# Moving the samples' chunk behind the first prompt chunk in the scans of a hybrid decoder layer

## The chip, the cores and the metric

One core of one Trainium2 chip. The metric is the device time of one execution in microseconds (us); lower is better. The kernel is written in Python with a tile framework: the program states tiles, pools and instructions, and a planner in the framework works out the order of the instructions on each engine.

## What is computed

One inference step of one decoder layer for 512 prompt tokens and 8 x 8 sample tokens that share the weights: a half-step SwiGLU FFN, one combined input projection, a Mamba-2 branch (SSD) and an attention branch side by side, a merge with an output projection, and a second half-step FFN. The change is in the SSD branch. Cut to it, the reference reads:

```python
xc, conv_new = causal_conv(xbc, conv_prev, conv_w, conv_b)      # depthwise, SiLU
acs = jnp.cumsum(dtc * A, axis=2)                               # inside a chunk of 128 tokens
cb = jnp.einsum('bclgn,bcsgn->bclsg', Cc, Bc)
y_diag = jnp.einsum('bclsgr,bcsgrp->bclgrp', cb[..., None] * decay, xdt)
states = jnp.einsum('bclgn,bclgr,bclgrp->bcgrpn', Bc, jnp.exp(acs[:, :, -1:] - acs), xdt)
# h = chunk_decay * h + states, from chunk to chunk
y_off = jnp.einsum('bclgn,bcgrpn,bclgr->bclgrp', Cc, h_prev, jnp.exp(acs))
y = (y_diag + y_off) + d_skip * x;  then y * silu(z) and a group RMSNorm
```

The prompt is four chunks of 128 tokens whose states form a chain. The samples are 8 sequences of 8 new tokens each with a state of its own from memory; the kernel takes all 64 tokens as one more chunk.

## The kernel before

All activations lie transposed, features on the 128 partitions and 576 tokens (512 prompt, 64 sample) on the free axis. Matrices are multiplied in three passes of split operands (`mm3`, L212, L215, L216: high x high, low x high, high x low), in two halves of 288 tokens. A weight tile is loaded by SP (`stage`, L164, four buffers), split by ScalarE (`whi`, L176) and by VectorE or GpSimd (`wlo`, L177). Results go to two PSUM banks `acc`; other PSUM rings are `tr`, `mm` and `pv`, two banks each.

The SSD branch goes in four groups g of eight heads. For each group `group_in(g)` projects six tiles (B, C and four tiles of x) and applies the conv in `conv_tile`: VectorE takes a projection out of `acc` (L1189, L1194, L1196), TensorE transposes the last columns into the same bank (L1202) and ScalarE copies them out (`tt`, L1204), VectorE adds the taps (L1215) and multiplies by the gate (L1217), GpSimd does so for the samples (L1220). `group_scan(g)` is the scan, and `group_out(g)` projects its result (L1474, L1477, L1481 take it out of `acc`). The emission order is scan g, `group_in(g+1)`, some gate tiles (`gate_tile`, evicted at L598; three behind scan 0, five behind scan 3), `group_out(g)`. The planner takes instructions by this order among those that are ready by its own planned times, so projections of the neighbouring groups stand between the pieces of a scan.

In a scan, `chunk(c, hst)` handles a chunk; c is 0 to 3 for the prompt and 4 for the samples:

- TensorE multiplies B and C (L1348) and VectorE masks it (L1349).
- For two sets of four heads, SP loads the cumulated decays to all partitions (`ab`, L1354, four buffers); ScalarE makes the ramps and the exponential (`dk`, L1359, L1360, four buffers) and VectorE multiplies by the masked scores (L1361). For chunks 1 to 3 ScalarE and GpSimd also make the factors for the state (L1363, L1364).
- TensorE transposes x (L1370) into an `mm` bank and VectorE scales it twice, `xdt` (L1373) and `xde` (L1375). TensorE transposes B (L1377) into another `mm` bank; ScalarE copies it (`bt`, L1380), or, for the samples, `operands` splits both and stores them with four transfers on ScalarE's queue for the last FFN (L1330 to L1340).
- TensorE does the product (L1386) and, for chunks 1 to 3, that with the state so far (L1390), both into a `pv` bank; VectorE adds the skip (L1392). For the prompt, `gate` loads z (L1309, one buffer), multiplies on GpSimd (L1311) and squares.

`carry` multiplies `xde` and `bt` (L1401, an `mm` bank) into the new state `hst` (L1404 for chunk 0, L1406 and L1407 behind it). `state` multiplies the samples' old states, loaded by SP (`hT`, L1413, three buffers), for each c (L1415). At the end of a scan the samples' part is put together (L1440, L1442) and gated, and `halves` splits the result for `group_out` (L1324, L1325).

Of the kernel before, what the change touches and what calls it, by code (L numbers as in the profile page):

```python
# [89 lines left out]
def ap3(ap, offset, dims):  # L90
    return bass.AP(tensor=ap.tensor, offset=ap.offset + offset, ap=[list(d) for d in dims])


def build(ctx, tc, A, O):
# [3 lines left out]
    def tl(pool, shape, dt=F32, tag=None, bufs=None):  # L98
        uid[0] += 1
        kw = {} if bufs is None else {"bufs": bufs}  # L100
        return pool.tile(shape, dt, tag=tag, name=f"{tag}_{uid[0]}", **kw)
# [23 lines left out]
    def C(n, rows=P):  # L125
        o, w = COFF[n]
        return cst[:rows, o - P:o - P + w]

    def bank(tag, bufs=None):
        return tl(sp, [P, 512], tag=tag, bufs=bufs)  # L130

    def tr():
        return bank("tr", 2)

    def sm():
        return bank("mm", 2)

    def pv():
        return bank("pv", 2)
# [1103 lines left out]
    with qyp:  # L1243
        with pool("yhl", reuse_waits="tile") as yhp:

            yhl = []
            for n, y in enumerate(yt):
                c = G.tensor_copy(y[:, NP:], ys[:, n // 4, n % 4, :])
# [32 lines left out]
    with pool("ssd", side="right", reuse_waits="tile") as wk:  # L1281
# [13 lines left out]
        def group_scan(g, bT, cT, xg):  # L1295
# [10 lines left out]
            def gate(o0, n):  # L1306

                zt = tl(xz, [P, 4, P], tag="zt", bufs=1)[:, :, :n]
                nc.sync.dma_start(out=zt, in_=zD[:, 4 * g:4 * g + 4, o0:o0 + n])  # L1309
                yv = xg[:, :, o0:o0 + n]  # L1310
                G.tensor_tensor(yv, yv, zt, ALU.mult)  # L1311
                q = tl(tp, [P, 4, P], tag="sq", bufs=1)[:, :, :n]
                act(q, yv, AF.Square)
                G.tensor_tensor(q[:, :2, :], q[:, :2, :], q[:, 2:, :], ALU.add)
                G.tensor_tensor(ysq[:, o0:o0 + n], q[:, 0, :], q[:, 1, :], ALU.add)

            def halves(half):

                for i in range(4):
                    if half == 0:  # L1320
                        yhl.append((tl(wo, [P, NT], F32R, tag="ygh", bufs=4), tl(wo, [P, NT], F32R, tag="ygl", bufs=4)))
                    w = P1[:, 24 + 4 * g + i:25 + 4 * g + i]
                    hi, lo = yhl[i][0][:, hs(half)], yhl[i][1][:, hs(half)]
                    act(hi, xg[:, i, hs(half)], AF.Copy, scale=w)  # L1324
                    V.scalar_tensor_tensor(lo, xg[:, i, hs(half)], w, hi.bitcast(F32), ALU.mult, ALU.subtract)  # L1325

            def operands(x, bp):

                xh = tl(wk, [NS, 512], F32R, tag="x4", bufs=3)
                act(xh, x, AF.Copy)  # L1330
                xl = tl(wk, [NS, 512], F32R, tag="x4", bufs=3)
                V.tensor_tensor(xl, x, xh.bitcast(F32), ALU.subtract)
                bh = tl(wk, [NS, P], F32R, tag="cbm", bufs=2)
                act(bh, bp, AF.Copy)
                bl = tl(wk, [NS, P], tag="cbm", bufs=2)
                V.tensor_tensor(bl, bp, bh.bitcast(F32), ALU.subtract)
                nc.scalar.dma_start(out=upxD[g, 0], in_=xh.bitcast(F32))
                nc.scalar.dma_start(out=upxD[g, 1], in_=xl.bitcast(F32))
                nc.scalar.dma_start(out=upbD[g, 0], in_=bh.bitcast(F32))
                nc.scalar.dma_start(out=upbD[g, 1], in_=bl)  # L1340

            def chunk(c, hst):

                n = P if c < 4 else NS
                o0 = c * P

                cbm = tr()
                mm(cbm[:n, :n], lhsT=bT[:, o0:o0 + n], rhs=cT[:, o0:o0 + n], start=True, stop=True)  # L1348
                V.tensor_tensor(cbm[:n, :n], cbm[:n, :n], C("mT") if c < 4 else C("smT", NS), ALU.mult)  # L1349
                abs_, dks = [], []  # L1350
                for r0 in (0, 4):
                    ab = tl(wk, [P, 4, P], tag="ab", bufs=4)
                    abv = ab[:n, :, :n]
                    nc.sync.dma_start(out=abv, in_=ap3(cumD, (g * 8 + r0) * NT + o0, [(0, n), (NT, 4), (1, n)]))  # L1354
                    dk = tl(wk, [P, 4, P], tag="dk", bufs=4)
                    dv = dk[:n, :, :n]
                    for r in range(4):
                        a0 = 64 + g * 8 + r0 + r
                        act(dv[:, r, :], abv[:, r, :], AF.Relu, bias=TT[c][:n, a0:a0 + 1], scale=-1.0)  # L1359
                    act(dv, dv, AF.Exp, scale=-1.0)  # L1360
                    V.tensor_tensor(dv, dv, cbm[:n, :n].unsqueeze(1).to_broadcast([n, 4, n]), ALU.mult)  # L1361
                    if 0 < c < 4:
                        act(ab, ab, AF.Exp)  # L1363
                        G.tensor_tensor(ab, ab, cT[:, o0:o0 + P].unsqueeze(1).to_broadcast([P, 4, P]), ALU.mult)  # L1364
                    abs_.append(ab)
                    dks.append(dk)

                t = sm()
                for i in range(4):
                    nc.tensor.transpose(t[:n, i * P:(i + 1) * P], xg[:, i, o0:o0 + n], ident)  # L1370
                xdt = tl(wk, [P, 8, 64], tag="xdt", bufs=2)
                tv = t[:n].rearrange("s (r p) -> s r p", p=64)
                V.tensor_tensor(xdt[:n], tv, TT[c][:n, g * 8:(g + 1) * 8].unsqueeze(2).to_broadcast([n, 8, 64]), ALU.mult)  # L1373
                xde = tl(wk, [P, 8, 64], tag="xde" if c < 4 else "x4", bufs=1 if c < 4 else 3)
                V.tensor_tensor(xde[:n], tv, wdec[:n, c, g * 8:(g + 1) * 8].unsqueeze(2).to_broadcast([n, 8, 64]), ALU.mult)  # L1375
                t = sm()
                nc.tensor.transpose(t[:n, :P], bT[:, o0:o0 + n], ident)  # L1377
                if c < 4:
                    bt = tl(wk, [P, P], tag="bt", bufs=1)
                    act(bt[:n], t[:n, :P], AF.Copy)  # L1380
                else:
                    bt = operands(xde.rearrange("s r p -> s (r p)")[:NS], t[:NS, :P])
                yb = pv()
                for r in range(8):
                    ov = yb[(r % 2) * 64:(r % 2 + 1) * 64, (r // 2) * n:(r // 2 + 1) * n]
                    own = mm(ov, lhsT=xdt[:n, r, :], rhs=dks[r // 4][:n, r % 4, :n], start=True, stop=not 0 < c < 4)  # L1386
                    if r == 0:
                        owns.append(own)
                    if 0 < c < 4:
                        mm(ov, lhsT=hst[:, r, :], rhs=abs_[r // 4][:, r % 4, :], start=False, stop=True)  # L1390
                for i in range(4):
                    V.scalar_tensor_tensor(xg[:, i, o0:o0 + n], xg[:, i, o0:o0 + n], dsk[:, 4 * g + i:4 * g + i + 1],  # L1392
                                           yb[:, i * n:(i + 1) * n], ALU.mult, ALU.add)
                if c < 4:
                    gate(o0, n)
                return xde, bt

            def carry(c, hst, xde, bt):

                s = sm()  # L1400
                mm(s, lhsT=bt, rhs=xde.rearrange("s r p -> s (r p)"), start=True, stop=True)  # L1401
                hn = tl(wk, [P, 8, 64], tag="hst", bufs=2)
                if c == 0:
                    act(hn.rearrange("n r p -> n (r p)"), s, AF.Copy)  # L1404
                else:
                    G.tensor_tensor(hn, hst, decb[:, c, g * 8:(g + 1) * 8].unsqueeze(2).to_broadcast([P, 8, 64]), ALU.mult)  # L1406
                    V.tensor_tensor(hn.rearrange("n r p -> n (r p)"), hn.rearrange("n r p -> n (r p)"), s, ALU.add)  # L1407
                return hn

            def state(h, i, ob):  # L1410

                hT = tl(wk, [P, 512], tag="hT", bufs=3)
                nc.sync.dma_start(out=hT, in_=hTD[h, 4 * g + i])  # L1413
                for b in range(4):
                    mm(ob[b * 32:(b + 1) * 32, :P], lhsT=cz[:, 4 * h + b, :], rhs=hT[:, b * P:(b + 1) * P], start=h == 0, stop=h == 1)  # L1415

            chunk(4, None)
            oo = tl(wk, [P, 512], tag="oo", bufs=1)
            hst = None
            for c in range(4):  # L1420
                hst = carry(c, hst, *chunk(c, hst))
                ob = pv()
                for h in range(2):
                    state(h, c, ob)
                act(oo[:, c * P:(c + 1) * P], ob[:, :P], AF.Copy)
                if c == 2 and g < 3:
                    halves(0)
# [159 lines left out]
```

## Time and profile before

| | |
|---|---|
| median of 3 runs | 1837.36 us (1836.68 to 1840.5) |
| profiled execution, its own time | 1829.29 us |
| its span, first to last instruction | 1827.4 us |
| granted TensorE clock, mean | 1.00 |
| TensorE busy (PE) | 1798.5 us, 98% |
| weight loads busy (PEld) | 1713.3 us, 94% |
| VectorE, ScalarE, GpSimd busy | 1014.7, 758.1, 630.6 us |

A row of the profile names the source line, the engine, the operation and the tiles. PE is TensorE's matmuls, PEld its weight loads, which overlap them; DVE is VectorE, ACT ScalarE, POOL GpSimd, and SPq, ACTq are the queues on which transfers are issued. Matmuls are pipelined, so a busy PE is not PE at its peak, and the distance between two starts says more than a matmul's own length. A matmul of plain f32 operands stands as two records.

### The profile page before, as it was taken

What the parts mean: (1) busy time and instruction counts of PE and PEld (TensorE: products, weight loads), DVE (VectorE), ACT (ScalarE), POOL (GpSimd) and SP (SyncE); (2) the same over time, 40 slices, a digit from 0 to 9 for tenths busy, and PEclk for the clock granted to TensorE, in tenths of its full rate; (3) what the DMA queues carried; (4) which work ended last, traced back from release to release, by engine and by line L of the source; (5) the groups of instructions that cost most, each with busy time, mean ns of one, the idle gap of its engine ahead of it and who ended that gap; (6) DMA issues with size and microseconds to landing.
All of it is one profiled execution on the core that took longest, in us unless ns stands there. A gap on an engine that the chain in (4) does not pass through costs nothing.

```text
span 1827.4 us, 38776 instructions
## 1 busy us (share of the span) xinstructions
PE 1798.5 (98%) x15315; PEld 1713.3 (94%) x15315; DVE 1014.7 (56%) x2259; ACT 758.1 (41%) x1598; POOL 630.6 (35%) x724
## 2 busy tenths in 40 slices
PE   8999999999999999999999999999999999999999
PEld 7999999999999888888998888888999999999998
DVE  4643334434426777775728857686675444444542
ACT  4333223334324565564427555555333333123322
POOL 0433002312322455453325454848452322002210
PEclk9999999999999999999999999999999999999999
DMA  5544443444546688774356554454473434543342
GB/s 164 161 120 138 129 134 109 124 137 133 120 132 197 201 243 240 244 231 158 89 164 183 153 139 112 124 151 138 153 215 93 127 116 130 152 139 110 111 124 66
DMA packets 297739, 269.72 MB, mean 148 GB/s; under 512 B 55084, under 2 KB 262108, under 8 KB 297404
## 3 DMA queue, kind: packets, MB, share of 16 engines
q1 hardware_dynamic: 229712, 184.16, 35.7%
q10 hardware_dynamic: 57844, 46.10, 8.2%
q0 software_dynamic: 10000, 36.97, 6.4%
q8 instruction: 121, 1.98, 0.5%
q14 instruction: 62, 0.51, 0.1%
HBM read 223.72 MB, written 38.73 MB: 144 GB/s over the span
## 4 chain that ended last, share of the span: by engine, by line
PE 88%; DVE 5%; DMA 3%; ACT 1%; issue 1%; POOL 1%; ACTq 0%; DVEq 0%; SPq 0%; POOLq 0%
PE acc L212 17%; PE acc L215 16%; PE acc L216 16%; PE pv L212 8%; PE pv L215 8%; PE pv L216 8%; PE tr L990 2%; PE tr L977 1%; PE mm L913 1%; PE pv L1386 1%; PE pv L944 1%; PE mm L931 1%; DVE kf L1215 1%; PE mm L1401 1%; PE pv L1028 1%
## 5 line engine op out<-in xcount | busy, mean ns | idle before, releaser
L176 ACT ACTIVATE whi<-stage 128x512 fp32r<-128x512 f32 (+2 forms) x474 | 294.3, 622 | 687.2 <-PE acc L215 589.1
L212 PE MATMUL acc<-xh,whi 128*128 128x288 f32 x1792 | 539.4, 301 | 11.1 <-DVE xr L1189 4.8
L215 PE MATMUL acc<-xl,whi 128*128 128x288 f32 x1792 | 530.4, 296 | 0.0
L216 PE MATMUL acc<-xh,wlo 128*128 128x288 f32 x1792 | 529.3, 295 | 0.0
L177 DVE TENSOR_TENSOR wlo<-stage,whi 128x512 fp32r<-128x512 f32 (+1 forms) x373 | 262.3, 703 | 257.1 <-ACT whi L176 235.0
L212 PEld LDWEIGHTS acc<-xh,whi 128*128 128x128 f32 x1792 | 336.4, 188 | 17.7 <-DVE xr L1189 7.2
L215 PEld LDWEIGHTS acc<-xl,whi 128*128 128x128 f32 x1792 | 336.6, 188 | 1.3 <-issue 1.2
L216 PEld LDWEIGHTS acc<-xh,wlo 128*128 128x128 f32 x1792 | 336.2, 188 | 0.9 <-issue 0.7
L353 POOL TENSOR_TENSOR u<-u,s 128x288 f32<-128x288 f32 x88 | 82.3, 936 | 433.9 <-DVE u L352 378.2
L177 POOL TENSOR_TENSOR wlo<-stage,whi 128x512 fp32r<-128x512 f32 (+1 forms) x101 | 133.9, 1326 | 276.3 <-ACT whi L176 243.3
L212 PE MATMUL pv<-xh,whi 128*128 128x288 f32 (+1 forms) x720 | 213.3, 297 | 0.6 <-ACT xh L227 0.6
L215 PE MATMUL pv<-xl,whi 128*128 128x288 f32 (+1 forms) x720 | 211.7, 294 | 0.0
L216 PE MATMUL pv<-xh,wlo 128*128 128x288 f32 (+1 forms) x720 | 211.6, 294 | 0.0
L212 PEld LDWEIGHTS pv<-xh,whi 128*128 128x128 f32 (+1 forms) x720 | 134.2, 186 | 1.2 <-ACT xh L227 0.8
L215 PEld LDWEIGHTS pv<-xl,whi 128*128 128x128 f32 (+1 forms) x720 | 134.1, 186 | 1.2
L216 PEld LDWEIGHTS pv<-xh,wlo 128*128 128x128 f32 (+1 forms) x720 | 134.0, 186 | 0.2
L212 PE MATMUL pv<-hh,whi 128*128 128x288 f32 x352 | 105.7, 300 | 0.0
L215 PE MATMUL acc<-hl,whi 128*128 128x288 f32 x352 | 104.1, 296 | 0.0
L212 PE MATMUL acc<-hh,whi 128*128 128x288 f32 x352 | 104.1, 296 | 0.0
L215 PE MATMUL pv<-hl,whi 128*128 128x288 f32 x352 | 104.1, 296 | 0.0
L216 PE MATMUL acc<-hh,wlo 128*128 128x288 f32 x352 | 104.1, 296 | 0.0
L216 PE MATMUL pv<-hh,wlo 128*128 128x288 f32 x352 | 103.7, 295 | 0.0
(370 smaller groups left out, 3560.1 us busy)
## 6 DMA issues: line engine op xcount, KB each, us to landing
stage<-in_w_in_dram SPq DMA_DIRECT2D x52, 512.0 KB
stage<-in_ffn_w_up_dram SPq DMA_DIRECT2D x44, 512.0 KB
stage<-in_ffn_w_gate_dram SPq DMA_DIRECT2D x43, 512.0 KB
stage<-in_ffn_w_down_dram SPq DMA_DIRECT2D x40, 512.0 KB
h<-in_state_ssm_dram SPq DMA_DIRECT2D x64, 256.0 KB
hTD<-hT ACTq DMA_DIRECT2D x32, 256.0 KB
pb<-pastD SPq DMA_DIRECT2D x32, 256.0 KB
ab<-cumD SPq DMA_DIRECT2D x32, 256.0 KB
```

Of the source, the lines that this page charges most:

```text
L176: act(hi, view, AF.Copy)
L177: e.tensor_tensor(lo, view, hi.bitcast(F32), ALU.subtract)
L212: begin = mm(out, lhsT=hi, rhs=a, start=first and i == 0, stop=False)
L215: mm(out, lhsT=hi, rhs=b, start=False, stop=False)
L216: end = mm(out, lhsT=lo, rhs=a, start=False, stop=last and i == n - 1)
L353: G.tensor_tensor(u, u, sil[half], ALU.mult)
L913: mm(s[:, :n], lhsT=q, rhs=ks[2 * self.p + e][:, :n], start=hl == 0, stop=hl == 1)
L931: nc.tensor.transpose(t[:, j * P:(j + 1) * P], lt[:, j * P:(j + 1) * P], ident)
L944: mm(self.ob[o:o + 32, i * P:(i + 1) * P], lhsT=vtok[j][:, v0:v0 + 32], rhs=self.pts[e][:, j * P:(j + 1) * P], start=j == 0, stop=j == i)
L977: nc.tensor.transpose(t[:, i * P:(i + 1) * P], kk[:, i, p * P:(p + 1) * P], ident)
L990: mm(s[kv * 32:(kv + 1) * 32, :], lhsT=self.q(kv), rhs=self.kT[kv // 2], start=True, stop=True)
L1028: mm(ob[kv * 32:(kv + 1) * 32, :64], lhsT=self.pt[:, i * P + kv * 32:i * P + (kv + 1) * 32], rhs=vv[:, i, kv * 64:(kv + 1) * 64], start=jq ...
```

## The change

The call for the samples' chunk is moved in each of the four scans: instead of ahead of the loop over the prompt's chunks it stands inside, behind `chunk(0)` and its `carry`, and ahead of the first pair of `state` calls. `chunk` and `carry` themselves are unchanged.

```diff
-            chunk(4, None)
             oo = tl(wk, [P, 512], tag="oo", bufs=1)
             hst = None
             for c in range(4):
                 hst = carry(c, hst, *chunk(c, hst))
+                if c == 0:
+                    chunk(4, None)
                 ob = pv()
                 for h in range(2):
                     state(h, c, ob)
```

## Rows read from the trace of the kernel before

**Rows 1.** The page: its part 1 (busy time of each engine, share of the span, instructions), and the first line of its part 4, which is the chain that ended last, by engine.

```profile
PE 1798.5 (98%) x15315; PEld 1713.3 (94%) x15315; DVE 1014.7 (56%) x2259; ACT 758.1 (41%) x1598; POOL 630.6 (35%) x724
...
PE 88%; DVE 5%; DMA 3%; ACT 1%; issue 1%; POOL 1%; ACTq 0%; DVEq 0%; SPq 0%; POOLq 0%
```

**Rows 2.** The view of windows: for each stretch of the span (us) its length, then busy time of PE, PEld, DVE, ACT and POOL with their numbers of instructions, granted clock, DMA share and GB/s. A stretch ahead of the scans, the four scans, and the first scan's dense part.

```profile
100.00:500.00 400.00, 399.17 (x3035) 396.86 (x3033) 158.37 (x296) 136.42 (x249) 90.99 (x95) 1.00 0.44 128
960.00:1310.00 350.00, 339.08 (x2807) 303.96 (x2806) 254.28 (x551) 200.02 (x488) 198.87 (x227) 1.00 0.50 143
970.00:1010.00 40.00, 39.30 (x379) 33.63 (x379) 37.98 (x73) 35.43 (x95) 29.18 (x31) 1.00 0.66 187
```

**Rows 3.** The waits of PE from 880 to 1320 us: who waited for whom, us in total, times, longest. The two largest.

```profile
PE acc L212 <- DVE xr L1189: 4.4, 7, 2.2
PE acc L212 <- ACT tt L1204: 3.7, 8, 1.4
```

**Rows 4.** The timeline of PE in the second scan (start us, us, engine, line, operation, out<-in, number merged): the product of the samples' chunk (64*64), the pieces of the first prompt chunk behind it, and projection matmuls between them.

```profile
1047.55 0.33 PE L1386 MATMUL pv<-dk,xdt 64*64 64x64 f32 x2
...
1049.37 0.29 PE L216 MATMUL acc<-ygh,wlo 128*128 128x288 f32 x1
1049.59 0.67 PE L1386 MATMUL pv<-dk,xdt 64*64 64x64 f32 x14
1050.19 0.33 PE L1377 MATMUL mm<-ident,bT 128*128 128x128 f32 x1
1050.28 0.38 PE L212 MATMUL acc<-ygh,whi 128*128 128x288 f32 x1
1050.50 0.30 PE L215 MATMUL acc<-ygl,whi 128*128 128x288 f32 x1
...
1052.05 0.87 PE L1386 MATMUL pv<-dk,xdt 128*64 128x128 f32 x10
...
1057.26 1.02 PE L1401 MATMUL mm<-xde,bt 128*128 128x512 f32 x2
...
1060.88 0.66 PE L1370 MATMUL mm<-ident,xg 128*128 128x128 f32 x4
```

**Rows 5.** The timelines of ACT and, in the last row, of POOL in the second scan.

```profile
1050.07 2.16 ACT L1359 ACTIVATE dk<-ab,TT 128x128 f32<-128x128 f32 x7 [1.23 <-PE pv L1386]
1052.13 0.26 ACT L1380 ACTIVATE bt<-mm 128x128 f32<-128x128 f32 x1
...
1059.08 0.59 ACT L1404 ACTIVATE hst<-mm 128x512 f32<-128x512 f32 x1
...
1058.15 2.54 POOL L1364 TENSOR_TENSOR ab<-ab,cT 128x512 f32<-128x512 f32 x2
```

**Rows 6.** Groups of instructions by line and form from 955 to 1330 us, for the forms of the samples' chunk (64 partitions or 64 columns), all four scans: VectorE's, then ScalarE's. Number, busy us, mean ns of one, idle time before them and what ended it.

```profile
L1332 DVE TENSOR_TENSOR x<-x,x 64x512 fp32r<-64x512 f32 x4 | 3.9, 976 | 0.0
...
L1392 DVE SCALAR_TENSOR_TENSOR xg<-xg,dsk,pv 128x64 f32<-128x64 f32 x16 | 3.4, 268 | 0.1
...
L1361 DVE TENSOR_TENSOR dk<-dk,tr 64x256 f32<-64x256 f32 x8 | 2.9, 399 | 0.0
...
L1375 DVE TENSOR_TENSOR x<-mm,wdec 64x512 f32<-64x512 f32 x4 | 2.7, 676 | 0.0
L1373 DVE TENSOR_TENSOR xdt<-mm,TT 64x512 f32<-64x512 f32 x4 | 2.7, 673 | 0.0
...
L1359 ACT ACTIVATE dk<-ab,TT 64x64 f32<-64x64 f32 x32 | 8.7, 336 | 12.7 <-DMA ab<-cumD 12.7
...
L1360 ACT ACTIVATE dk<-dk 64x256 f32<-64x256 f32 x8 | 3.3, 409 | 0.1
```

**Rows 7.** The timeline of PE, rows with idle time ahead of them (in brackets, with what ended it), at the heads and ends of the scans.

```profile
973.12 0.40 PE L212 MATMUL acc<-xh,whi 128*128 128x288 f32 x1 [0.70 <-DVE xr L1189]
...
1013.07 0.40 PE L212 MATMUL acc<-xh,whi 128*128 128x288 f32 x1 [2.21 <-DVE xr L1189]
...
1128.62 0.40 PE L212 MATMUL acc<-xh,whi 128*128 128x288 f32 x1 [0.58 <-ACT tt L1204]
...
1197.05 0.40 PE L212 MATMUL acc<-xh,whi 128*128 128x288 f32 x1 [1.37 <-ACT tt L1204]
...
1228.00 0.41 PE L212 MATMUL acc<-xh,whi 128*128 128x288 f32 x1 [0.33 <-DVE xr L1189]
```

**Rows 8.** Timelines of the first scan: PE's products of the first and the third prompt chunk, VectorE's decays of the third chunk, a split and an eviction at the scan's end; and of the last scan: VectorE's last splits and last eviction of a gate tile.

```profile
981.28 0.66 PE L1386 MATMUL pv<-dk,xdt 128*64 128x128 f32 x8
...
994.93 0.45 PE L1386 MATMUL pv<-dk,xdt 128*64 128x128 f32 x4
...
989.43 1.27 DVE L1361 TENSOR_TENSOR dk<-dk,tr 128x512 f32<-128x512 f32 x2
...
1006.60 2.65 DVE L1325 SCALAR_TENSOR_TENSOR ygl<-xg,P,ygh 128x288 fp32r<-128x288 f32 x3
...
1012.58 0.45 DVE L1189 TENSOR_TENSOR xr<-acc,rbc 128x288 f32<-128x288 f32 x1
...
1304.83 1.36 DVE L1325 SCALAR_TENSOR_TENSOR ygl<-xg,P,ygh 128x288 fp32r<-128x288 f32 x3
...
1312.30 0.46 DVE L598 SCALAR_TENSOR_TENSOR kf<-acc,rbc 128x288 f32<-128x288 f32 x1 [0.38 <-PE acc L216]
```

**Rows 9.** The waits of SP's queue from 955 to 1310 us, its load of z.

```profile
SPq L1309 <- POOL xg L1311: 13.3, 9, 3.4
```

## The prediction

> **What bounds the kernel now.** I read the page first. TensorE is busy in 98% of the span and makes up 88% of the chain that ended last [rows 1]. The four scans lie between 960 and 1310 us, so I cut the span there by the view of windows [rows 2]: in those 350 us the matmul rows are busy for 339.08 and leave 10.92 us free. Before the scans, from 100 to 500 us, it is 0.83 us in 400. So the scans hold most of the idle time left in the middle of the kernel, and it is 0.6% of the whole.
>
> The waits of TensorE in that stretch [rows 3] say what the idle time is. No wait is on a product of a scan. TensorE waits for VectorE to evict a conv tile (L1189, 4.4 us in 7 waits) and for ScalarE to take the small transposed block out of the same bank (L1204, 3.7 us in 8). Both hold one of the two `acc` banks that the projections use. The scans don't starve TensorE themselves; they load VectorE and ScalarE, and where the end or the head of a scan meets the conv tiles of the next group, an eviction stands in a queue.
>
> **Where the samples' chunk stands now.** In scan 1 [rows 4] its product (L1386, 64x64) starts at 1047.55, is broken off by twelve projection matmuls and ends at 1050.19. Only then comes the transposition of B for the prompt's first chunk (L1377, 1050.19), that chunk's product at 1052.05, and its state's product (L1401) at 1057.26. The second chunk's transpositions follow at 1060.88. So the chain through the state is behind the samples' chunk on TensorE by one or two of the slots that the projections leave. On ScalarE the copy that the state needs (L1380) is queued behind 2.16 us of ramps (L1359) that the samples' product set free [rows 5].
>
> **The change part by part.** Nothing is removed or added: 20 calls of `chunk` stay 20, with the same instructions, shapes and transfers. What moves is the samples' chunk, one per scan, behind `chunk(0)` and `carry(0)` and in front of the first `state` pair.
>
> *Work moved.* Per scan on VectorE [rows 6]: two products of decays and masked scores of 0.399, the two scaled copies of x 0.673 and 0.676, the split of one 0.976, and four additions of 0.268, together 4.2 us beside small pieces. On ScalarE: eight ramps of 0.336 and two exponentials of 0.409, together 3.5 us beside copies. On TensorE sixteen recorded matmuls, of which fourteen took 0.67 us [rows 4], and a few transpositions. It also moves its two loads of `ab` on SP's queue and four stores on ScalarE's. All of it lies beside projection matmuls, which fill TensorE from `group_out` of the group before and `group_in` of the next. Summed, the moved work changes the time by 0; without that cover the 4.2 us of VectorE would be exposed in each scan, 17 us in all, but it is covered before and after.
>
> *What the state gains.* The first chunk's transposition of B can take the slot of the samples' product, 1047.55 to 1050.19 in scan 1, against 1050.19 now, and the state's product can come 2.6 us or one to two slots earlier, up to 1057.26 - 1050.19 = 7.1 us. But the second chunk isn't bound by the state alone. Its transpositions take the two `mm` banks; before it the ring must serve two tiles of the samples' chunk, two of the first chunk and one of the state. These five turns come before it in either order. The state was ready at 1059.67 (1059.08 + 0.59) and the transpositions ran at 1060.88; its second row of factors on GpSimd (L1364, 1058.15 and 2.54 long) was done at 1060.69 [rows 4, 5]. Neither would come earlier because the state does. I take 0 of the 7.1 us as passed on to the scan's end, with 7.1 us a scan as the other bound.
>
> *What the conv evictions gain.* At the heads of the scans both chunks' early work stands in VectorE's queue in front of evictions. Five waits there, from 0.70 us at 973.12 to 0.33 at 1228.00 and with the 0.58 at 1128.62 among them, are together 2.29 us [rows 7]. The samples' chunk and the first one go through the same steps, so the samples' chunk is about half of what stands there, and some of its work is now planned later: I take half, -1.1 us; bounds 0 and -2.29.
>
> *What TensorE's stream loses.* A scan piece put between projection matmuls costs more than its own length. In [rows 4] projections start 0.13 us apart; from the last one before a piece to the piece it is 0.22 (1049.37 to 1049.59), and behind it the first takes 0.22 (1050.28 to 1050.50), so an interruption costs 0.09 + 0.09, say 0.2 us. Now the samples' product shares a slot with the first chunk's transposition. Moved into the middle of the scan it may want a slot of its own: one more interruption in each of four scans, +0.8 us, bounds -0.8 (one fewer) and +2.4 (three more).
>
> *The queues.* SP's queue is served in order, and so is ScalarE's, which issues the four stores. On SP the samples' two loads of `ab` move behind the first chunk's load of z (L1309), which has a single buffer and waited up to 3.4 us on GpSimd [rows 9]; behind it stand weight stages too, but that load was there before. So the samples' ramps may begin 3.4 us later; they have until the scan's end, and I take 0. On ScalarE the four stores are issued behind the state's copy instead of ahead of it; nothing reads them before the last FFN. The `ab` buffers number four, two to a chunk, and neither the samples' nor the first chunk uses them in a product, so they come free after the ramps in either order. The `dk` buffers also number four. Now the second chunk's ramps wait for the samples' product and the third chunk's for the first one's; afterwards it is the other way round. The tightest is scan 0: the first product ends at 981.94, the third chunk's pair of decays is done at 990.70 and that chunk's product starts at 994.93, 4.2 us of cover [rows 8]. I take 0, with the loss worked out below as the bound.
>
> Sum: 0 + 0 - 1.1 + 0.8 + 0 = -0.3 us against the profiled execution's own 1829.29 (its span 1827.4 and 1.9 us around it). The runs shown have a median of 1837.36, some 8 us above the profiled one and so another level; the difference is carried over: 1837.36 - 0.3 = 1837.0.
>
> The Trainium skill, "Perfetto Trace Analysis", section "Identifying the Most-Contended Engine", speaks against taking the busy matmul rows as full: it says that matmul busy time is a poor measure of what is left and that weight-load busy time is the better one. Here weight loads are busy 303.96 of 350 us in the scans, 87%, against 99% from 100 to 500 us [rows 2], so by this rule 46 us are open where the matmul rows show 10.92. The trace agrees that the scans run less densely, since the pieces of a scan cost the interruptions priced above; by that rule the sum would still be -0.3, because no order of the same pieces takes their own length away, but the case for a gain is wider than the idle time alone would make it.
>
> **The rivals.** About 0.2%, 3.7 us, is what a measurement of this kernel can tell from no change.
>
> *Null (my forecast):* engines swap two pieces of work of about one size, every ring is turned as often, time 1837.0, own range 1833.7 to 1841.0.
>
> *Faster: the state's lead is passed on.* If the scan's chain does follow the state, each scan ends 2.6 us or more earlier and its last splits (L1325) leave VectorE before the conv evictions come. The two largest waits are such meetings: 2.21 us at 1013.07, where the eviction at 1012.58 stood behind 2.65 us of splits, and 1.37 us at 1197.05, on ScalarE's small block [rows 7, 8]. With both gone and the rest of the sum: -2.21 - 1.37 - 0.3 = -3.9, 1833.5; with all 8.1 us of the two wait groups in [rows 3] gone, 1829.3. For it: ScalarE's queue really has the state's copy behind the ramps. Against it: the five turns of the `mm` ring, and projections that outrank the scan's pieces.
>
> *Slower: the samples' chunk comes late in scan 0.* There VectorE and ScalarE have little slack: from 970 to 1010 us they are busy 37.98 and 35.43 of 40 us [rows 2]. If the samples' product there ends later than 981.94 + 4.2 = 986.2 us, the third chunk's ramps wait for `dk`, and scan 0 ends later by the excess. Its splits then fall further into the conv tiles; the 2.21 us wait grows by what is late, and as scans 1 and 2 end in the same way their 0.58 and 1.37 us waits grow too. At 1.5 us each, three meetings are +4.5 and with three more interruptions a scan +2.4: up to +6.9, middle +4.7, 1842. Scan 3 adds nothing: its last split ends at 1306.19 and the last covering gate tile is evicted at 1312.30, 6 us of cover [rows 8].
>
> **How the numbers follow.** Null 0.53, faster 0.26, slower 0.21. The faster case is a little likelier than the slower one, since the chain that ends the scan is put first and the moved chunk has until the scan's end. The range 1830.5 to 1843.5 takes in the middles of both rivals and leaves out the far end of each. Faster 0.26, same 0.53, slower 0.21.
>
> **What would show it.** In the changed kernel the 64x64 product should start behind the first 128x128 product in each scan, and L1401 of the first chunk earlier relative to it. Right: L1370 and L1386 of the second chunk no earlier relative to the end of the gate tiles or conv tiles, idle time of TensorE from 960 to 1310 us within 2 us of 10.92. Wrong to the fast side: the waits at L1189 and L1204 fall from 8.1 us below 4. Wrong to the slow side: waits of the third chunk's ramps on a samples' product, or L1189 waits above 7 us. What would upset all of it is the planner: the order on each engine is worked out from emission order and planned times, so a small shift could reorder weight loads far from the scans.

## The result, and the profile after

The changed kernel took 1841.11 us (median of 20 runs, 1837.76 to 1847.12) against 1837.03 for the kernel before (20 runs beside it, 1833.49 to 1840.77): a ratio of 1.0026, 95% interval 1.0018 to 1.0033. It is slower by 4.1 us. On another chip (e5 below) the same pair gave 1.0012 (1.0003 to 1.0021). The profiled execution of after took 1847.12 us, its span 1845.3: the longest of its 20 runs, while before's profiled one, 1829.29, is shorter than any of the 20 beside it. The two profiles are thus 17.8 us apart where the medians are 4.1 apart, and they serve here to find places, not the size. One run of e12 (5139 us) and one of e16 (2852 us) are left out of the ratios and means below.

The page of after, its part 1, answers to [rows 1]:

```profile
PE 1807.2 (98%) x15315; PEld 1721.8 (93%) x15315; DVE 1020.4 (55%) x2259; ACT 760.2 (41%) x1598; POOL 636.3 (34%) x724
```

The counts of instructions are the same on every engine, so nothing was added. PE is busy for 8.7 us longer with the same 15315 rows: 4.8 of these lie ahead of the scans, where the clock is 1.00 in both, and 3.9 in the stretch of the scans that is defined below. The windows of after, the scans and then six slices of 5 us (columns as in [rows 2]):

```profile
960.00:1310.00 350.00, 334.72 (x2749) 302.20 (x2748) 248.76 (x521) 193.87 (x475) 201.08 (x226) 0.98 0.52 142
985.00:990.00 5.00, 3.44 (x17) 3.44 (x18) 4.38 (x8) 4.33 (x13) 1.17 (x2) 0.72 0.78 204
990.00:995.00 5.00, 5.00 (x51) 4.46 (x50) 3.86 (x12) 2.54 (x6) 0.89 (x1) 0.94 0.59 153
1045.00:1050.00 5.00, 5.00 (x28) 5.00 (x27) 4.18 (x12) 1.18 (x3) 0.00 (x0) 0.66 0.27 91
1215.00:1220.00 5.00, 2.43 (x14) 1.71 (x13) 3.75 (x5) 3.16 (x7) 4.69 (x8) 0.93 0.97 286
1220.00:1225.00 5.00, 5.00 (x22) 5.00 (x23) 3.10 (x8) 1.33 (x2) 0.00 (x0) 0.50 0.22 75
1225.00:1230.00 5.00, 5.00 (x35) 4.81 (x35) 3.60 (x10) 1.91 (x4) 3.06 (x6) 0.89 0.21 59
```

Two things are new. The idle time of PE is 15.28 us of 350 instead of 10.92. And the granted clock, 1.00 throughout the scans before, falls in six slices, in one of them to half (0.50 is 1.2 GHz for the whole slice). Summed as 5 us x (1 - clock), the six slices lose 6.8 us. The only other slice of the execution below 0.97 is its last one (0.89; the last of before has 0.81).

The waits of PE from 880 to 1320 us, which answer to [rows 3]:

```profile
PE mm L268 <- POOL ssq L1315: 3.1, 2, 2.6
PE acc L212 <- ACT tt L1204: 2.7, 6, 1.4
PE acc L212 <- DVE xr L1189: 2.6, 4, 1.5
PE mm L1370 <- ACT hst L1404: 2.4, 1, 2.4
PE acc L1202 <- DVE xr L1196: 2.2, 3, 1.0
PE tr L1436 <- ACT oo L1426: 1.5, 1, 1.5
```

The conv tiles' two waits fell from 8.1 to 5.3 us together, but a third one, L1202 for L1196, is new with 2.2 us, so that the conv waits are 0.6 us less in all. The two long waits that before doesn't have are those for the copy of the first state (L1404) and for the samples' sum of squares (L1315). The timeline of PE shows them, each with what follows; the first fence is scan 0, the second the end of scan 2:

```profile
978.33 1.02 PE L1401 MATMUL mm<-xde,bt 128*128 128x512 f32 x2
979.18 0.60 PE L1370 MATMUL mm<-ident,xg 128*64 128x128 f32 x4
...
983.86 0.27 PE L1377 MATMUL mm<-ident,bT 128*64 128x128 f32 x1 [0.44 <-DVE x L1375]
986.56 0.66 PE L1370 MATMUL mm<-ident,xg 128*128 128x128 f32 x4 [2.43 <-ACT hst L1404]
986.97 0.40 PE L212 MATMUL acc<-xh,whi 128*128 128x288 f32 x1
...
987.65 0.44 PE L212 MATMUL acc<-xh,whi 128*128 128x288 f32 x1
987.89 0.44 PE L215 MATMUL acc<-xl,whi 128*128 128x288 f32 x1
```

```profile
1219.82 0.69 PE L268 MATMUL mm<-ssq,cst 128*128 128x64 f32 x2 [2.57 <-POOL ssq L1315]
...
1221.62 0.44 PE L216 MATMUL acc<-xh,wlo 128*128 128x288 f32 x1
1221.86 0.44 PE L212 MATMUL acc<-xh,whi 128*128 128x288 f32 x1
```

Behind both waits the projections start 0.24 us apart instead of 0.133: half the clock. The slices behind the first lose 1.7 us and those around the second 3.4. The remaining 1.7 us, in the slice from 1045, follow neither of them: TensorE's waits just ahead of that slice are 0.66 and 0.25 us. Why the first wait is there stands in ScalarE's timeline:

```profile
980.92 1.26 ACT L1359 ACTIVATE dk<-ab,TT 128x128 f32<-128x128 f32 x4
...
982.21 1.05 ACT L1359 ACTIVATE dk<-ab,TT 64x64 f32<-64x64 f32 x4
...
983.68 1.05 ACT L1359 ACTIVATE dk<-ab,TT 64x64 f32<-64x64 f32 x4
984.64 0.87 ACT L1213 ACTIVATE kf<-xr,P,P 128x600 f32<-128x600 f32 x1
985.42 0.61 ACT L1360 ACTIVATE dk<-dk 128x512 f32<-128x512 f32 x1
985.94 0.57 ACT L1404 ACTIVATE hst<-mm 128x512 f32<-128x512 f32 x1
```

The state's product had ended at 979.35, but its copy ran at 985.94, 6.6 us later. ScalarE had no pause in between; in front of the copy stood the first chunk's second set of ramps (128x128) and its exponentials, two weight splits, a conv step, and the samples' ramps (the 64x64 rows), which held the engine for 1.9 us. So the samples' ramps are not the whole of the delay, but 1.9 us is most of the wait of 2.43 that came of it. Until the copy ran, the state kept its `mm` bank. The samples' x took the other bank (979.18) and their B came next (983.86), behind the scaling that freed that bank; the second chunk's x then needed the bank of the state. In the kernel before, the second chunk's x came straight behind the state's product and did not need that bank, as PE's timeline of before shows (first fence). The state's copy was late there too, 2.5 us behind its product's end, but nothing on TensorE waited for it (second fence, ScalarE):

```profile
977.87 1.02 PE L1401 MATMUL mm<-xde,bt 128*128 128x512 f32 x2
978.73 0.60 PE L1370 MATMUL mm<-ident,xg 128*128 128x128 f32 x4
```

```profile
981.40 0.59 ACT L1404 ACTIVATE hst<-mm 128x512 f32<-128x512 f32 x1
```

How long the scans take can be read without the drift ahead of them, from the last `sq` tile that VectorE takes out of `acc` ahead of scan 0 to the last eviction of the merged projection behind scan 3. The timelines of VectorE, before and then after:

```profile
960.13 0.46 DVE L1276 SCALAR_TENSOR_TENSOR sq<-kf,acc 128x288 f32<-128x288 f32 x1 [0.30 <-PE acc L216]
...
1389.97 0.46 DVE L1529 SCALAR_TENSOR_TENSOR accs<-acc,accs 128x288 f32<-128x288 f32 x1 [0.37 <-PE acc L216]
```

```profile
969.70 0.46 DVE L1276 SCALAR_TENSOR_TENSOR sq<-kf,acc 128x288 f32<-128x288 f32 x1 [0.30 <-PE acc L216]
...
1407.88 0.46 DVE L1530 SCALAR_TENSOR_TENSOR accs<-acc,accs 128x288 f32<-128x288 f32 x1 [0.38 <-PE acc L216]
```

That is 429.84 us before and 438.18 after, +8.34. The other 9.6 us between these two executions (969.70 - 960.13) lie ahead of the change and don't come from it: in e5, the same kernel as after, the stretch starts at 960.94. Its length there is 435.04, so one kernel's stretch differs by 3 us between two profiles. I use this stretch, "the region", in every experiment.

### The profile page after: what moved, and what is told of

Same layout as the page of the kernel before. It is cut to its first block, busy times and chain, and to the rows that moved or that the text cites. A ratio compares the mean times of both kernels' runs of the same rounds, so it can differ in the third digit from the quotient of the medians.

```text
span 1845.3 us, 38787 instructions
## 1 busy us (share of the span) xinstructions
PE 1807.2 (98%) x15315; PEld 1721.8 (93%) x15315; DVE 1020.4 (55%) x2259; ACT 760.2 (41%) x1598; POOL 636.3 (34%) x724
```

## The experiments

Theory A: the cost is the two long waits of TensorE, at scan 0's head and scan 2's end, and the lower clock behind them. Rivals: B, each scan costs a quarter; C, any new order that the planner makes is worth some tenths of a per cent either way, and this was a bad one; D, the samples' chunk itself comes late.

All results in one table. The ratio is to the runs of before on the same chip and is not the quotient of the two medians; the region and what the clock lost are from one profiled execution each (slices of 5 us below 0.97); the last column is the mean over the runs of the span times (1 - mean granted clock), where the clock is given to 0.001, a step of 1.8 us. The chips differ: the first two rows are one chip, e1 to e4 another, and so are e5 to e8, e9 to e12 and e13 to e16.

| kernel | median us | ratio, 95% | region us | lost there | lost, mean of runs |
|---|---|---|---|---|---|
| before | 1837.03 | 1 | 429.84 | 0 | 1.7 to 2.5 beside e1 to e16 |
| the change | 1841.11 | 1.0026 (1.0018-1.0033) | 438.18 | 6.8 | 5.1 |
| e1 scan 0 only | 1837.90 | 1.0009 (0.9996-1.0023) | 434.93 | 3.5 | 4.0 |
| e2 scan 2 only | 1839.80 | 1.0013 (1.0001-1.0026) | 436.80 | 3.4 | 3.5 |
| e3 scans 1 and 3 | 1832.38 | 0.9981 (0.9970-0.9993) | 425.84 | 0 | 2.0 |
| e4 later squares | 1837.03 | 1.0000 (0.9988-1.0011) | 431.46 | 3.4 | 3.4 |
| e5 the change again | 1835.29 | 1.0012 (1.0003-1.0021) | 435.04 | 5.1 | 4.3 |
| e6 copy on VectorE | 1831.36 | 0.9983 (0.9974-0.9993) | 432.07 | 5.1 | 3.2 |
| e7 e4 and e6 | 1832.46 | 0.9999 (0.9990-1.0008) | 429.45 | 1.7 | 3.5 |
| e8 busy wait | 1837.43 | 1.0023 (1.0013-1.0032) | 433.62 | 1.7 | 3.5 |
| e9 as e3 | 1833.49 | 0.9986 (0.9977-0.9995) | 427.93 | 1.7 | 1.7 |
| e10 e3 and e6 | 1840.94 | 1.0032 (1.0021-1.0043) | 437.22 | 6.9 | 3.9 |
| e11 before, copy on VectorE | 1837.69 | 1.0014 (1.0005-1.0023) | 431.37 | 0 | 2.7 |
| e12 as e6 | 1836.33 | 1.0006 (0.9997-1.0016) | 429.82 | 1.7 | 3.5 |
| e13 before, xde first | 1839.23 | 1.0017 (1.0008-1.0026) | 434.70 | 1.7 | 3.3 |
| e14 change on e13 | 1841.10 | 1.0027 (1.0016-1.0038) | 435.84 | 1.7 | 2.9 |
| e15 before, scores late | 1836.24 | 1.0007 (0.9998-1.0016) | 429.73 | 0 | 1.7 |
| e16 change on e15 | 1839.21 | 1.0023 (1.0011-1.0036) | 433.93 | 3.4 | 4.8 |

**Where the cost lies: e1 to e3.** The moved call in some scans only, the old place in the others; for e1

```diff
+            if g != 0:
+                chunk(4, None)
...
-                if c == 0:
+                if c == 0 and g == 0:
                     chunk(4, None)
```

e2 has 2, and e3 has 1 and 3, in place of 0.

> The samples' chunk is moved in scan 0 alone; scans 1 to 3 have it in front as before. Theory A (two places: TensorE's wait of 2.43 us for the state's copy at the head of scan 0, and its wait of 2.57 us for the samples' squares at the end of scan 2, each followed by a stretch at the lower clock): about half of the 4.1 us that the whole change costs, +1.5 to +3 us against before, mean granted clock some 0.998 to 0.999, and the wait of L1370 for L1404 in the trace. Rival B (a quarter of the cost in each scan, by interruptions or lateness): +1 us, clock 1.000 with no wait above 1.5 us. Rival C (any new order planned from the same emission is as good as another, the loss is luck of the planner in the late scans): 0 +-1 us.

> The samples' chunk is moved in scan 2 alone. Theory A: +1.5 to +3 us, the wait of L268 for the samples' squares (L1315) above 2 us at the end of scan 2 and a stretch at the lower clock behind it. Rival B: +1 us, no such stretch. Rival C: 0 +-1 us.

> The samples' chunk is moved in scans 1 and 3, not in 0 and 2. Theory A: 0 +-1 us, clock 1.000. Rival B: half of the whole cost, +2 us. Rival C: anything between -2 and +3 us with no place of its own.

In e1 PE waits 2.42 us for the first state's copy, and the slice behind has a clock of 0.74: the first half of theory A, as far as the trace goes. The time, 1.0009, is in A's range, but its interval takes in 1; and half of the 3.5 us that the clock lost lies elsewhere, behind a wait of 2.13 us at 1268.83. The second half did not show in e2. The wait for the samples' squares is not there; waits of 2.21 and 2.15 us for conv evictions (L1189) have a clock of 0.66 behind them. In e3, with the change in the other two scans, the kernel is faster than before, by more than A, B or C had expected. So B falls: it is not a quarter in each. But e2 says that the place of the second long wait belongs to one order rather than to scan 2.

**Taking the waits away: e4 to e7.** e4 lets the matmul on the samples' squares be planned behind one more conv tile, e6 copies the first state on VectorE, e7 does both, e5 is the change unaltered:

```diff
-    def rowscale(s, inv, r, first=None):
+    def rowscale(s, inv, r, first=None, second=None):
...
-                behind(m2, first)
+                behind(m2, second or first)
...
-            rg = rowscale(ysq, 1.0 / 512, ysq, convs[6 * g + 7][3]) if g < 3 else None
+            rg = rowscale(ysq, 1.0 / 512, ysq, convs[6 * g + 7][3], convs[6 * g + 8][3]) if g < 3 else None
```

```diff
-                    act(hn.rearrange("n r p -> n (r p)"), s, AF.Copy)
+                    V.tensor_copy(hn.rearrange("n r p -> n (r p)"), s)
```

> The change as it is, and the second product of the group norm (L268) is held on TensorE behind one more conv half of 24 projection matmuls, so that the samples' squares are there when its turn comes; TensorE's order differs from the changed kernel in nothing but three places. Theory A: the 2.57 us wait and the stretch at the lower clock behind it go, -2.5 to -4 us against the changed kernel, so +0.5 to +2 us against before. Rival B: no more than the wait's excess over what it was before, -1 us. Rival C: 0 against the changed kernel, +4 against before.

> The changed kernel itself on this chip, as the measure for the three that follow. Both theories: +3 to +5 us against before, mean granted clock near 0.997, waits of 2.4 us (L1370 for L1404) and 2.6 us (L268 for L1315).

> The change, with the copy of the first state (L1404) made by VectorE instead of ScalarE, where it stood behind the samples' ramps. Theory A (long single waits of TensorE and the lower clock behind them are the cost): the 2.43 us wait at the head of scan 0 falls below 1 us, the clock stays up there, and the time is 1.5 to 3.5 us below the changed kernel's; the wait at the end of scan 2 stays. Theory D (the samples' chunk itself is late and the copy only shows it): the same wait reappears at the next tile of the ring, under 1 us gained.

> The change with both mends: first state copied by VectorE, and L268 held behind 24 more projection matmuls. Theory A: both long waits gone, clock above 0.998, time from 2 us above to 2 us below before. Theory D: still +2 to +3 us above before.

In e4 the wait of 2.57 us and the fall behind it are gone, and the region is 431.46; the wait for the copy stays, with its fall, 3.4 us. In e6 and e7 the wait for the copy is gone and L1370 waits 0.93 us for VectorE instead. The change itself cost less on this chip, 1.9 us by the medians where 3 to 5 were expected. Each edit alone brings the change to before or below, as A says. e6 is 4.2 +- 1.4 us below e5 by their means, on one chip, which D did not allow. e4 ran on another chip than the changed kernel did, and its interval touches that of e5, so its gain is less sure; and it keeps the wait at scan 0 and its fall and still isn't slower than before. Both edits together are no better than either. In e6's profile the clock still lost 5.1 us, though no wait is above 1.4, and the second long wait is gone too, for which e6 did nothing. So the sizes do not add up as A has them, and C could have made e6's gain as well.

**Filling the wait: e8.** Four products whose result nothing reads (128x384, each two records) stand behind the first matmul of the squares in scan 2, to keep TensorE busy where it waited:

```diff
-    def rowscale(s, inv, r, first=None):
+    def rowscale(s, inv, r, first=None, busy=0):
...
-            t2 = sm()
+            t2, fill = sm(), []
+            fill += [mm(t2[:, NS:NS + 384], lhsT=C("one"), rhs=s[:, :384], start=True, stop=True) for _ in range(busy)]
...
-                behind(m1, first)
-                behind(m2, first)
+                [behind(m, first) for m in (m1, m2)] + [behind(m, m1) for m in fill]
...
-            rg = rowscale(ysq, 1.0 / 512, ysq, convs[6 * g + 7][3]) if g < 3 else None
+            rg = rowscale(ysq, 1.0 / 512, ysq, convs[6 * g + 7][3], 4 if g == 2 else 0) if g < 3 else None
```

> The change, with four products of no use (128x384, f32) put on TensorE ahead of L268 in the group norm of group 2, so that TensorE computes while it would wait for the samples' squares; nothing else is taken away, and they cost about as much TensorE time as the 2.57 us wait. If the lower clock behind the wait is part of the cost: 1 to 3.5 us below the changed kernel, clock 1.00 between 1200 and 1240 us of the profile. If only the idle time counts: 0 to +1 us against the changed kernel.

The windows of e8:

```profile
1200.00:1210.00 10.00, 10.00 (x61) 8.20 (x60) 8.72 (x18) 6.07 (x13) 7.20 (x10) 1.00 0.86 236
1210.00:1220.00 10.00, 8.17 (x61) 7.79 (x60) 9.69 (x29) 3.30 (x7) 2.54 (x6) 1.00 0.13 32
```

The clock holds at 1.00 there; in e5 the slice behind this wait (1210 to 1215) had 0.66. But the kernel is not faster: 1.0023, and by the means 1.5 +- 1.5 us above e5. The useless products take TensorE's time themselves, 2.74 us where the wait was 2.57, as PE's timeline of e8 shows, and the next conv eviction is waited for 1.83 us.

```profile
1205.16 2.74 PE L268 MATMUL mm<-ssq,cst 128*128 128x384 f32 x8
```

It is a miss as a mend, and it goes against A's price for the clock: of the two readings expected it is nearer to the one in which only the idle time counts. Since another wait came at the same time, it does not decide between them.

**Is it the move or the order? e9 to e12.** e9 is e3 again, e10 adds the copy on VectorE to it, e11 is before with that copy alone, e12 is e6 again (the diffs are those above).

> The samples' chunk behind the first chunk in scans 1 and 3, ahead of the loop in scans 0 and 2, as in e3, on another chip. Theory A (the cost sits in scans 0 and 2, the move is worth something in 1 and 3): ratio again 0.997 to 0.9995, no wait of TensorE over 1 us that is not at a conv eviction, mean granted clock in the runs no lower than that of before. Theory C (e3 was the luck of one order against one sample of before): 1.000 within 0.001.

> e9 with the first state's copy (L1404) on VectorE in all four scans. Theory A (the copy on ScalarE costs where the samples' ramps stand in front of it, and that is scan 0 of the whole change alone): nothing to gain here, 1.000 beside e9 within 0.001. The rival (the copy on VectorE is worth 2 us by itself in any order): about 0.997 against before, 2 us below e9.

> The kernel before with only that copy moved to VectorE: the control of e6. Theory A: e6 gained 0.29% on the change (0.9983 against 1.0012) because it takes away the 2.43 us wait that the change made; before has no such wait, so here 0.999 to 1.001. The rival (the copy is better on VectorE anyway): 0.998 or less.

> e6 once more, on another chip, beside its control: theory A 0.9975 to 0.9995 again; if e6 was the luck of one chip, 1.000 or above.

e9 confirms e3, 0.9986, though one wait that is not at a conv eviction is above 1 us (1.27, at the end of scan 3). e12, the same kernel as e6 on another chip, does not confirm it: 1.0006 after 0.9983, with 1 inside its interval, which by its own expectation speaks for the luck of one chip. e11 and e10 are outside what A expected, and go against the rival too: the copy on VectorE costs 0.14% on before and 0.46% on e9 (1.0032 / 0.9986), where no wait was there to take away. In e10 a new one has come, in PE's timeline:

```profile
1115.39 0.61 PE L212 MATMUL acc<-xh,whi 128*128 128x288 f32 x1 [3.69 <-ACT tt L1204]
1115.80 0.44 PE L215 MATMUL acc<-xl,whi 128*128 128x288 f32 x1
```

So C is partly true: an edit that only reorders is worth up to some tenths of a per cent. A needs a test over several orders.

**The change on other orders: e13 to e16.** Two neutral edits, each without the change (e13, e15) and with it (e14, e16). One emits `xde` ahead of `xdt`, the other emits the product of B and C and its mask behind the first four heads' ramps:

```diff
-                V.tensor_tensor(xdt[:n], tv, TT[c][:n, g * 8:(g + 1) * 8].unsqueeze(2).to_broadcast([n, 8, 64]), ALU.mult)
                 xde = tl(wk, [P, 8, 64], tag="xde" if c < 4 else "x4", bufs=1 if c < 4 else 3)
                 V.tensor_tensor(xde[:n], tv, wdec[:n, c, g * 8:(g + 1) * 8].unsqueeze(2).to_broadcast([n, 8, 64]), ALU.mult)
+                V.tensor_tensor(xdt[:n], tv, TT[c][:n, g * 8:(g + 1) * 8].unsqueeze(2).to_broadcast([n, 8, 64]), ALU.mult)
```

```diff
-                cbm = tr()
-                mm(cbm[:n, :n], lhsT=bT[:, o0:o0 + n], rhs=cT[:, o0:o0 + n], start=True, stop=True)
-                V.tensor_tensor(cbm[:n, :n], cbm[:n, :n], C("mT") if c < 4 else C("smT", NS), ALU.mult)
...
                     act(dv, dv, AF.Exp, scale=-1.0)
+                    if r0 == 0:
+                        cbm = tr()
+                        mm(cbm[:n, :n], lhsT=bT[:, o0:o0 + n], rhs=cT[:, o0:o0 + n], start=True, stop=True)
+                        V.tensor_tensor(cbm[:n, :n], cbm[:n, :n], C("mT") if c < 4 else C("smT", NS), ALU.mult)
```

> The kernel before, with the two scaled copies of x in each chunk emitted in the other order (xde ahead of xdt). The work is the same, but 706 rows of TensorE's order differ from before. Theory A (the cost belongs to the move): this has no reason to differ from before, 0.9995 to 1.0005. Theory C (an order of this kernel is worth 0.1 to 0.3% either way by itself): outside that, of either sign.

> The whole change on top of e13. Theory A: 0.1 to 0.25% above e13, with TensorE's wait for the first state's copy (L1370 behind L1404) again above 2 us in scan 0. Theory C: between 0.3% below and 0.3% above e13, and that wait need not be there.

> The kernel before, with the product of B and C and its mask emitted behind the loads and ramps of the first four heads instead of ahead of them, in every chunk: 1267 rows of TensorE's order differ. Theory A: 0.9995 to 1.0005. Theory C: outside that, of either sign.

> The whole change on top of e15. Theory A: 0.1 to 0.25% above e15, with the wait for the first state's copy above 2 us in scan 0. Theory C: between 0.3% below and 0.3% above e15.

The change costs 0.10% on e13 (1.0027 / 1.0017) and 0.16% on e15 (1.0023 / 1.0007), beside 0.12 and 0.26% on before. By the spread of the runs the means differ by 2.2 +- 1.4 us (e14, e13) and 3.0 +- 2.1 us (e16, e15), so the change is slower in all four pairs. With the copy on VectorE, in the one order measured, it is not: e12 against e11 is -0.08% (1.0006 / 1.0014), -1.8 +- 2.0 us. And the wait comes back. PE's timelines of e14 and of e16 (whose lines are one higher):

```profile
983.18 1.12 PE L1370 MATMUL mm<-ident,xg 128*128 128x128 f32 x4 [2.24 <-ACT hst L1404]
```

```profile
979.48 1.12 PE L1371 MATMUL mm<-ident,xg 128*128 128x128 f32 x4 [2.42 <-ACT hst L1405]
...
980.63 0.44 PE L215 MATMUL acc<-xl,whi 128*128 128x288 f32 x1
```

It stands in all seven profiles of kernels that have the moved call in scan 0 and the copy on ScalarE (the change, e5, e1, e4, e8, e14, e16), 2.24 to 2.43 us long and each time with a lower clock behind it. It is in none of the other eleven. The wait for the samples' squares is in the change, e5 and e16, but not in e14: it depends on the order. And another order of the kernel before can cost as much by itself: e13 is 0.17% slower, which A did not expect, and its profile has a wait of 4.09 us for the squares (L266) with no change made. e15's 0.07% can't be told from no difference.

What stands, then: the wait at scan 0 comes with the move, and the move's cost is there on three orders with the copy on ScalarE and not on the one with the copy on VectorE. That this wait is the cost is argued from its size: alone it is as long as the smaller of the losses, 1.9 us, and with the clock behind it (1.7 to 3.4 us) it covers the largest, 4.1. e4, which has it and is no slower than before, shows that the rest of an order can make up for it. No run kept the copy on ScalarE and took only the samples' ramps from in front of it. The second wait belongs to orders. How much of the 0.12 to 0.26% would be left under an average order is open. e3's gain from scans 1 and 3 was shown for one order, on two chips. As far as measured, e3 is the fastest place for the call, and beats both kernels.

## Why the prediction failed

**What bounds the kernel.** It read "No wait is on a product of a scan" off before and took it as a property of the scans ("The scans don't starve TensorE themselves"). That was not so even in before, whose next row in the same view is a wait of the product of B and C:

```profile
PE tr L1348 <- POOL cT L1220: 1.4, 2, 0.7
```

In after two of the four largest waits are the scans' own.

**Work moved: 0.** This held as work (the counts are the same), but the cover was named as projection matmuls. The samples' ramps on ScalarE were covered only as long as nothing that TensorE needed next stood behind them.

**What the state gains: 0 of 7.1 us. The failed step.** It said of the `mm` ring: "These five turns come before it in either order." The count is right; what matters is which tile has to leave which bank. Before, the second chunk's x followed the state's product in scan 0 after 0.86 us (977.87, 978.73) and did not have to wait for the state's copy. After, the samples' two tiles come between, and the second chunk's x gets the bank that the state's copy has to empty: TensorE stands for 2.43 us where the prediction has 0. The prediction had noticed on [rows 5] that the copy of B, which the state needs, is queued behind ramps in the old order, and counted it as a possible gain; it didn't ask which work the state's own copy would stand behind in the new one. That the state's lead is not passed on was nearly right: in scan 0, counted from the start of the region, the state's product came 9.1 us earlier, its copy 5.0 and the second chunk's x 1.7; in scan 1 the second chunk's x starts at 1081.83, 21 us behind its place in [rows 4], and only 9.6 of these were there ahead of the scans.

**Conv evictions: -1.1 (0 to -2.29).** The waits for L1189 and L1204 fell by 2.8 us, but with the new one at L1202 the conv waits are 0.6 us less in all: the sign was right and the size inside the range. **Interruptions: +0.8.** They can't be told apart from the rest, but the sign is in doubt: the region at full clock (438.18 - 6.8 = 431.4, e5 435.04 - 5.1 = 429.9) is 0.1 to 1.5 us longer than before's 429.84, with the 5.0 us of the two new waits in it, so something else became shorter by 3.5 us or more. The sum of everything but the clock was thus nearly 0, as forecast, with other terms.

**The queues: 0.** SP's queue and the four stores did nothing that shows, as predicted. ScalarE's waits for products ahead of prompt ramps, the `dk` ring, became longer in scans 1 to 3, before and then after, but no wait of TensorE is seen to follow from them:

```profile
ACT dk L1359 <- PE pv L1386: 3.1, 3, 1.2
```

```profile
ACT dk L1359 <- PE pv L1386: 5.0, 3, 1.7
```

The prediction weighed ScalarE's queue for its stores alone and not for the copy.

**The missing term.** TensorE's clock is in no term of the prediction; before shows 1.00 throughout the scans. In the profiled pair it is 6.8 of the 8.3 us, 1.7 of them behind the wait of 2.43; over the runs the change loses 4.3 us to it in e5 against 2.5 of before beside it, 1.8 of the 2.4 us between their means, and e16 loses 3.1 us more than e15, all of their difference. In e14 it is none of it (2.9 against 3.3), so this term is not there on every order.

**The rivals.** The slower one had the time (1842) but not the mechanism, and its time was met by luck: its condition was a samples' product in scan 0 that ends later than 986.2, and it ended at 993.41, which is 983.8 when the 9.6 us ahead of the scans are taken off; L1189's longest wait fell from 2.21 to 1.46 us. The faster one's sign, conv waits below 4 us, did not come (5.3). The upset named last, that the planner reorders far more than the edit, was right: a neutral edit moved the kernel by 0.17% (e13).

## What to carry to other kernels

When a piece of work is moved in front of a copy that empties a shared PSUM bank, ask who takes that bank next: equal counts of turns do not mean equal waits. A gain or loss of 0.2% after an edit that lets a planner reorder everything is no proof of the edit's mechanism; try it on two or three other orders, with a control for each, and look for the wait that comes back every time. And in a kernel that runs at full clock, allow for a new wait of TensorE above 2 us to cost more than its own length: in 15 of 22 such waits here a lower clock followed.

## What the hardware showed that was not expected

A wait of TensorE of some 2 us inside a full stretch can be followed by matmuls at half the clock. Of the 22 waits of 2.1 us or more that the profiles hold in the scans, 15 had a slice below 0.97 behind them and 7 had not, and the same wait in the same kernel goes either way. The timeline of PE in e3 and then in e9, the same program on two chips:

```profile
1019.56 0.40 PE L212 MATMUL acc<-xh,whi 128*128 128x288 f32 x1 [2.21 <-DVE xr L1189]
1019.80 0.29 PE L215 MATMUL acc<-xl,whi 128*128 128x288 f32 x1
1019.93 0.29 PE L216 MATMUL acc<-xh,wlo 128*128 128x288 f32 x1
```

```profile
1020.13 0.61 PE L212 MATMUL acc<-xh,whi 128*128 128x288 f32 x1 [2.22 <-DVE xr L1189]
1020.54 0.44 PE L215 MATMUL acc<-xl,whi 128*128 128x288 f32 x1
1020.78 0.44 PE L216 MATMUL acc<-xh,wlo 128*128 128x288 f32 x1
```

Behind the first the projections go on 0.13 us apart; behind the second 0.24 us apart, and the slice from 1020 to 1025 has a clock of 0.66, 1.7 us lost, nearly as much as the wait. In the rows above a fall cost 1.7 to 3.4 us. It also came where no wait was above 1.4 us but several stood close together (e6: 0.81, 0.93 and 1.34 us between 975 and 981, then 0.53 from 980 to 985). The mean granted clock of an execution differs by 0.001 to 0.004 between runs of one kernel, some 2 to 7 us, which is as much as the change itself.
